# A 3x3 convolution with 2x2 max pooling: another sequence of steps and another order of all instructions

## The chip, the cores and the metric

The kernel runs on one core of a Trainium2 chip. A core has TensorE (PE in the profile; its weight loads are PEld), VectorE (DVE), ScalarE (ACT), GpSimd (POOL) and SyncE (SP), which issues most of the transfers. Each engine executes its own list of instructions strictly in the order in which the program wrote them, and waits at an instruction until the semaphores it needs have come. The metric is the device time of one execution in microseconds (us).

## What is computed

The reference, cut to what matters; the inputs are float32, x is 16 x 64 x 64 x 64, the weight 128 x 64 x 3 x 3, the output 16 x 128 x 32 x 32:

```python
x_pad = np.pad(x, ((0, 0), (0, 0), (pad, pad), (pad, pad)), mode='constant')
...
conv[b, co] += weight[co, ci, kh, kw] * x_pad[b, ci, kh:kh+h, kw:kw+w]
...
output[b, c, i, j] = np.max(conv[b, c, i*pool_size:(i+1)*pool_size,
                                          j*pool_size:(j+1)*pool_size])
```

## The kernel before

**Steps.** Two images lie on the 128 partitions, 64 input channels each (h = 0 and h = 1 in the names). A pair of images is cut into four quarters of 16 input rows, which give 8 rows of pooled output. A quarter of a pair is one step; there are 8 x 4 = 32 steps. Pooling takes the maximum of two neighbouring rows y0 and y1, and later of two neighbouring columns. With g0, g1, g2 for the three rows of the filter, and a, b, c, d for the rows 2i-1 to 2i+2 of the input,

- a K step (13 of them) makes five products: A = (g2-g1) c + g0 a (PAa and PAb), B = (g0-g1) b + g2 d (PBa and PBb), and R = g1 (b+c) (PR); max(y0, y1) is max(A, B) + R. It needs the rows in bf16 (tile kx, cast by the transfer that GpSimd issues) and one row operation, ks = b+c;
- a W step (19) makes four: P2 = (g0+g2-g1)/2 (c-b), P0 = g0 (a-c), P3 = g2 (d-b), P1 = (g0+g2+g1)/2 (b+c); y0 = P2+P0+P1 and y1 = P3-P2+P1, so the maximum is max(P2+P0, P3-P2) + P1. It needs the rows in float32 (tile wx, from transfers that SP issues) and four row operations: we = c-b, wz = a-c, wy = d-b, ws = b+c.

`SEQ` is the sequence of K and W steps; it also decides in which quarter of which pair each lies (`place`, lines 45 to 51).

**Products.** Each product is three matmuls for the three columns of the filter, on 64 partitions, into one bank of PSUM. There are eight banks (`acc`). A token such as `P1.2.0+PBa.3.1:6` in the order is a group of six matmuls: product P1 of W step 2, image 0, in turn with PBa of K step 3, image 1; ":6" names the bank that is taken. The two images' matmuls use different halves of TensorE and run side by side. Below, a *group* is such a token.

**What the other engines do for a step**, by the names in the order (capitals for K, small letters for W):

- ScalarE: `EV`/`ev` copies the first accumulator (A, or P2+P0) to SBUF and frees its bank (line 290); `SE` writes -P2 into a second bank, to which P3 is added (295); `OD`/`od` copies the odd columns to SBUF (303).
- VectorE: `MX`/`mx` takes the maximum of the second accumulator and the copy (299), in place, and only then may PR or P1 be added to it; `CM`/`cm` takes the maximum of even and odd columns, which frees the bank (327), and the second of two images stores the step (344). `KS`, `S` and `E` are the row operations ks, ws and we (260).
- GpSimd: `Z`, `Y` and `e` are wz, wy and we. A row operation there first waits for the last VectorE operation within SBUF that the order has before it (`on_gpsimd`, lines 81 to 83). `L0` to `L5` issue the loads of kx from K step 2 on, two K steps each (L5 one); L0 waits for KS.0.
- SP: `LD.n` loads W step n. It waits for nothing but its place in SP's list, except that LD.1 waits for GM, LD.2 for E.0 and LD.3 for E.1 (line 371); the stores stand in the same list.

**The weights.** At the start wraw, the filter, lands; g0, g1 and g2 are cast, D2 = g2-g1, D0 = g0-g1, GS = g0+g2, and from it GM and GP are made. Each is turned by four transposes on TensorE (`TD2` and so on) into a bank and copied out (`VD2` and so on) to wt. "/V", "/A" and "/P" name VectorE, ScalarE or GpSimd for an operation that can go to either.

**The first rows.** The rows of K step 0 land in float32 (kfirst) and are cast by `XO1`, `XO` (odd rows) and `XE` (even rows); those of K step 1 land in ksecond (`KX2`, issued behind D2) and are cast by `X1` and `X2`.

**The order** of all this is written out by hand as one string of 577 tokens, `ORDER`, from line 420 on; the loop behind it issues them one by one.

```python
    for s in ORDER.split():
        act_left[0] -= on_act(s)
        if s[0] == "P":
...
            for matmuls in zip(*made):
                for matmul in matmuls:
                    matmul()
```

The stores of the last two steps go out per image; those made when ScalarE has at most one of its own operations left go in turn to ScalarE's queue and SP's, behind ScalarE's last operation (lines 309 to 320).

Of the kernel before, what the change touches and what calls it, by code (L numbers as in the profile page):

```python
# [10 lines left out]
def kernel(  # L11
# [404 lines left out]


    ORDER = """  # L420
        D0/V g2 g1/P D2 g0 TD0:1 GS/V TD2:4 KX2 XO1/A TG1:0 VD2/V TG0:2 GP/V XO/A TG2:3 VG0/A
# [9 lines left out]
        od.1.1 MX.2.0 SE.2.0:2 PAb.3.0+P3.2.1 cm.1.1 Y.3 MX.2.1 PR.2.0+P2.3.1:4 EV.3.0 mx.2.1
        P0.2.0+PAa.3.1:0 OD.2.0 S.3 P2.3.0:5+P1.2.1 ev.2.0 CM.2.0 e.4 P3.2.0+PAb.3.1 od.2.1 SE.3.1:3 cm.2.1
        PBa.3.0:7+PR.2.1 mx.2.0 SE.3.0:1 Z.4 PBb.3.0+P0.3.1 OD.2.1 P0.3.0+P3.3.1 CM.2.1 ev.3.1 MX.3.0 Y.4
        P1.2.0+PBa.3.1:6 ev.3.0 LD.8 mx.3.1 P2.4.0:4+PBb.3.1 EV.3.1 E.5 od.2.0 PR.3.0+P1.3.1 SE.4.0:5 KS.4
        cm.2.0 P3.3.0+PAa.5.1:0 Y.5 OD.3.0 MX.3.1 od.3.1 P0.4.0+PAb.5.1 mx.3.0 P3.4.0+PR.3.1 Z.5 cm.3.1
        ev.4.0 P1.3.0+P2.4.1:2 EV.5.1 mx.4.0 OD.3.1 PAa.4.0:3+PAa.4.1:4 L2 S.4 SE.4.1:0 PAb.4.0+PAb.4.1
        od.3.0 CM.3.0 Y.6 CM.3.1 P1.4.0+P0.4.1 EV.4.0 cm.3.0 P2.5.0:6+P3.4.1 LD.9 od.4.0 S.5 EV.4.1
        PBa.4.0:3+P2.5.1:7 cm.4.0 e.7 ev.4.1 PBb.4.0+PBa.4.1:1 mx.4.1 SE.5.0:2 PAa.5.0:4+PBb.4.1 SE.5.1:5
        KS.5 MX.4.0 PAb.5.0+P1.4.1 e.6 MX.4.1 P0.5.0+P0.5.1 EV.5.0 PR.4.0+P3.5.1 S.6 ev.5.1 Z.6
        P3.5.0+P2.6.1:4 ev.5.0 mx.5.1 od.4.1 PBa.5.0:7+PR.4.1 OD.4.0 mx.5.0 Y.7 PBb.5.0+P1.5.1 CM.4.0 OD.4.1  # L440
# [6 lines left out]
        P3.7.0+PR.6.1 od.7.1 S.9 ev.8.1 P0.8.0+P3.8.1 Z.9 cm.7.1 mx.7.0 P3.8.0+PAa.7.1:5 ev.8.0 mx.8.1
        P1.7.0+PAb.7.1 OD.6.1 Y.9 OD.6.0 mx.8.0 P2.9.0:0+P1.8.1 EV.7.1 CM.6.0 e.10 P1.8.0+P2.9.1:2 CM.6.1
        od.8.1 SE.9.0:5 cm.8.1 PAa.9.0:1+PBa.7.1:6 SE.9.1:3 S.10 P0.9.0+PBb.7.1 od.8.0 KS.7 od.7.0
        P3.9.0+P0.9.1 cm.8.0 ev.9.0 Y.10 MX.7.1 PAb.9.0+P3.9.1 ev.9.1 mx.9.0 PBa.7.0:7+P2.10.1:0 EV.9.0 Z.11  # L450
# [5 lines left out]
        od.10.0 P0.11.0+P2.12.1:1 mx.11.1 OD.8.0 Z.13 cm.10.0 P3.11.0+PR.8.1 ev.11.0 CM.8.0
        P2.12.0:3+P1.11.1 OD.8.1 mx.11.0 e.13 SE.12.1:2 PBa.9.0:7+PAb.9.1 CM.8.1 od.11.1 P1.11.0+P3.12.1
        cm.11.1 EV.9.1 KS.9 PBb.9.0+P0.12.1 SE.12.0:6 S.13 od.11.0 P2.13.0:0+PBa.9.1:5 E.14 ev.12.1
        P0.12.0+PBb.9.1 Y.14 cm.11.0 SE.13.0:1 mx.12.1 P3.12.0+P2.13.1:4 ev.12.0 MX.9.1 Z.14 P0.13.0+P1.12.1
        SE.13.1:3 MX.9.0 P3.13.0+PR.9.1 ev.13.0 mx.12.0 e.15 PR.9.0+P0.13.1 OD.9.1 mx.13.0 P1.12.0+P3.13.1  # L460
        CM.9.1 OD.9.0 Y.15 ev.13.1 CM.9.0 P1.13.0+P2.14.1:0 od.12.1 mx.13.1 od.12.0 PAa.11.0:4+P2.15.1:5
        od.13.0 Z.15 cm.12.0 SE.14.1:7 PAb.11.0+P1.13.1 cm.12.1 cm.13.0 PAa.10.0:6+P0.14.1 od.13.1 E.16
        SE.15.1:1 PAb.10.0+P3.14.1 S.15 ev.14.1 P2.14.0:2+P0.15.1 EV.11.0 cm.13.1 S.14 L5 P2.15.0:0+P3.15.1
        ev.15.1 LD.18 e.17 mx.14.1 PBa.10.0:4+PAa.11.1:3 EV.10.0 mx.15.1 SE.14.0:5 PBb.10.0+PAb.11.1
        SE.15.0:6 S.17 P0.14.0+P1.14.1 EV.11.1 KS.10 P0.15.0+P1.15.1 Z.17 MX.10.0 ev.14.0 P3.15.0+PAa.10.1:3
        od.15.1 ev.15.0 cm.15.1 P3.14.0+PAb.10.1 Y.16 od.14.1 mx.15.0 PR.10.0+PBa.10.1:2 EV.10.1 mx.14.0
        Y.17 P2.17.0:0+PBb.10.1 OD.10.0 cm.14.1 P1.15.0+P2.16.1:3 SE.17.0:1 MX.10.1 Z.16 P1.14.0+PAa.12.1:7
        CM.10.0 od.15.0 cm.15.0 P0.17.0+PR.10.1 od.14.0 SE.16.1:4 cm.14.0 P2.16.0:6+PAb.12.1 ev.17.0 S.18
        PBa.11.0:5+P0.16.1 OD.10.1 KS.11 EV.12.1 P3.17.0+P2.17.1:0 S.16 SE.16.0:7 PBb.11.0+P3.16.1 CM.10.1
        e.18 ev.16.1 mx.17.0 P0.16.0+PBa.11.1:2 SE.17.1:3 MX.11.0 P1.17.0+PBb.11.1 Y.18 ev.16.0  # L470
# [77 lines left out]
```

## Time and profile before

| | |
|---|---|
| median of 3 runs | 105.12 us (104.89 to 105.39) |
| the profiled execution | 104.92 us |
| its span, first to last instruction | 103.1 us |
| TensorE busy | 97.2 us (94%) |
| VectorE busy | 90.5 us (88%) |
| ScalarE busy | 81.8 us (79%) |
| GpSimd busy | 67.1 us (65%) |
| granted TensorE clock | full throughout |
| HBM read, written | 17.14 MB, 8.39 MB |

All times below are from the start of the span, in us. A line of a timeline gives the start, the length, the engine, the line of the program, the operation, what it wrote and read, and in brackets how long the engine stood idle before it and what ended that. Operations of one engine overlap a little at their ends, and a matmul is shown longer (0.38) than the time after which the next one is issued (0.11), since they are pipelined.

### The profile page before, as it was taken

The numbers are of one execution on the slowest core, as the hardware profiler recorded it, in microseconds if no ns is written. First come the engines' busy times: TensorE is split into PE (matmuls) and PEld (weight loads), VectorE is DVE, ScalarE is ACT, GpSimd is POOL, SyncE is SP. The second block draws the span as 40 slices with busy tenths as digits, with TensorE's granted clock in tenths as the row PEclk, the third lists the DMA queues.
The fourth block names the chain that finished last, engine by engine and source line by source line (L and its number), as shares of the span: only waits on it lengthen the run. The fifth ranks groups of instructions, "written<-read, shape, count | busy, mean of one in ns | idle before, by whom it ended". The sixth has DMA issues, their size and how long they took to land.

```text
span 103.1 us, 2507 instructions
## 1 busy us (share of the span) xinstructions
PE 97.2 (94%) x888; PEld 55.8 (54%) x888; DVE 90.5 (88%) x178; ACT 81.8 (79%) x177; POOL 67.1 (65%) x76
## 2 busy tenths in 40 slices
...
GB/s 56 353 294 240 214 197 287 223 314 210 404 303 261 152 214 266 245 227 157 213 211 366 317 225 311 199 257 230 379 180 156 236 126 68 199 41 97 113 217 88
DMA packets 12925, 22.81 MB, mean 221 GB/s; under 512 B 1008, under 2 KB 9200, under 8 KB 12912
## 3 DMA queue, kind: packets, MB, share of 16 engines
...
q8 instruction: 7, 0.11, 0.5%
q10 hardware_dynamic: 144, 0.13, 0.4%
q14 instruction: 6, 0.05, 0.2%
HBM read 17.14 MB, written 8.39 MB: 247 GB/s over the span
## 4 chain that ended last, share of the span: by engine, by line
PE 86%; DMA 7%; DVE 2%; ACT 1%; DVEq 0%; issue 0%
PE acc L202 86%; DMA ksecond<-in_x_dram 5%; DMA wraw<-in_weight_dram 3%; DVE wq L391 1%; ACT kx L348 1%; DVE wq L356 0%; DVE o L327 0%; ACT od L303 0%; DVEq L543 0%
## 5 line engine op out<-in xcount | busy, mean ns | idle before, releaser
L202 PEld LDWEIGHTS <-wt 64*128 64x128 bf16 x852 | 53.1, 94 | 38.4 <-issue 1.2
L202 PE MATMUL acc<-kx,wt 64*128 64x504 bf16 (+5 forms) x318 | 57.5, 369 | 0.5 <-ACT kx L348 0.5
L299 DVE TENSOR_TENSOR acc<-acc,ev 128x512 f32<-128x512 f32 x64 | 42.4, 693 | 3.1 <-PE acc L202 2.0
L290 ACT COPY ev<-acc 128x512 f32<-128x512 f32 x64 | 36.6, 592 | 6.2 <-PE acc L202 5.6
L260 POOL TENSOR_TENSOR wz<-wx 128x512 bf16<-128x512 f32 x19 | 24.2, 1274 | 10.8 <-DVE ks L260 4.5
L202 PE MATMUL acc<-wy,wt 64*128 64x504 bf16 (+1 forms) x114 | 29.6, 377 | 0.0
L202 PE MATMUL acc<-wz,wt 64*128 64x504 bf16 (+1 forms) x114 | 29.2, 377 | 0.0
L260 POOL TENSOR_TENSOR wy<-wx 128x512 bf16<-128x512 f32 x19 | 24.1, 1273 | 7.7 <-PE acc L202 3.0
L202 PE MATMUL acc<-we,wt 64*128 64x504 bf16 (+1 forms) x114 | 29.1, 377 | 0.0
L202 PE MATMUL acc<-ws,wt 64*128 64x504 bf16 (+1 forms) x114 | 29.1, 376 | 0.0
L327 DVE TENSOR_TENSOR o<-acc,od 128x256 f32<-128x256 f32 x64 | 25.3, 417 | 2.7 <-ACT od L303 2.3
L303 ACT COPY od<-acc 128x256 f32<-128x256 f32 x64 | 23.0, 382 | 4.4 <-PE acc L202 3.3
L295 ACT ACTIVATE acc<-acc 128x512 f32<-128x512 f32 x38 | 22.0, 586 | 3.4 <-DVE o L327 1.9
L202 PE MATMUL acc<-ks,wt 64*128 64x504 bf16 (+1 forms) x78 | 19.7, 377 | 0.0
L260 POOL TENSOR_TENSOR we<-wx 128x512 bf16<-128x512 f32 x11 | 14.0, 1270 | 5.1 <-PE acc L202 3.4
L260 DVE TENSOR_TENSOR ws<-wx 128x512 bf16<-128x512 f32 x19 | 15.1, 798 | 0.0
L260 DVE TENSOR_TENSOR we<-wx 128x512 bf16<-128x512 f32 x8 | 6.1, 767 | 0.0
L260 DVE TENSOR_TENSOR ks<-kx 128x512 bf16<-128x512 bf16 x13 | 5.4, 419 | 0.1
L105 POOL DMA_DIRECT2D kx<-in_x_dram x6 | 3.5, 589 | 0.0
L482 PE MATMUL acc<-const-bfloat16-1.0 128*128 128x512 bf16 x6 | 2.7, 623 | 0.8 <-PEq L529 0.8
L356 DVE TENSOR_TENSOR wq<-wraw 128x192 bf16<-128x192 f32 x1 | 0.5, 507 | 2.4 <-DMA wraw<-in_weight_dram 2.4
L164 PEld LDWEIGHTS <-wq 128*128 128x128 bf16 x28 | 1.7, 102 | 1.5 <-issue 0.8
...
## 6 DMA issues: line engine op xcount, KB each, us to landing
...
```

The source lines that it names most:

```text
L105: return nc.gpsimd.dma_start(out=ktile(i)[:, lo:hi, :], in_=rows_of(p, lo, hi))
L164: nc.tensor.transpose(turned_rows(m)[:, j, :], wq[:, BLOCKS[m] - 1 + j : BLOCKS[m] + 1 + j, :].rearrange("a b c -> a (b c)"), ident,)
L202: lambda kw=kw, o0=o0, o1=o1, c0=c0, c1=c1: nc.tensor.matmul(dst[:, i0:i1, o0:o1], wt[lo : lo + CI, m0 + kw - h, :], rows(lo, i0, i1, c0, c1),
L260: return engine.tensor_tensor(out=r, in0=t[:, f + a : f + a + 2 * R - 1 : 2, :], in1=t[:, f + b : f + b + 2 * R - 1 : 2, :], op=op,)
L290: nc.scalar.copy(out=ev[g], in_=acc[:, ta[g]])
L295: nc.scalar.mul(acc[:, t], acc[:, ta["w", i, h]], -1.0)
L299: nc.vector.tensor_tensor(out=t, in0=t, in1=ev.pop(g), op=MAX)
L303: nc.scalar.copy(out=od[g], in_=acc[:, tb[g], :, 1::2])
L327: nc.vector.tensor_tensor(out=o[:, h], in0=acc[:, tb[g], :, 0::2], in1=od.pop(g), op=MAX,)
L348: nc.scalar.copy(out=out, in_=in_)
L391: "D2", on_vector(nc.vector.tensor_sub(out=slots(D2), in0=g2, in1=g1))
L482: warm = nc.tensor.matmul(acc[:, n], src[:, 0:128], src, start=True, stop=True, skip_group_check=True)
```

## The change

`SEQ` begins with K and W in turn for eight steps instead of six, and a few W and K change places further on; the numbers of K steps (13) and W steps (19) stay. `ORDER` is a new permutation of the same 577 steps with other banks, in which these operations go to another engine:

- from VectorE to GpSimd: D0 and GP; from GpSimd to ScalarE: g1;
- from VectorE to ScalarE: VG1 and XE; from ScalarE to VectorE: VD0, VG2, VGM, XO and X1;
- we of eleven W steps on VectorE (`E`) and eight on GpSimd (`e`), instead of eight and eleven.

At the start D2 stands ahead of D0 on its engine's list, and L0 ahead of Z.0. At the end P1.18.0 and P1.18.1 form the last group, where before PR.12.0 and P1.18.1 did. The diff, with lines of the order left out:

```diff
-    SEQ = "KWKWKWWKWKWWKWKWWKWKWWKWKWWKWWKW"
+    SEQ = "KWKWKWKWWKWKWWKWWKWKWWKWWKWKWWKW"
...
     ORDER = """
-        D0/V g2 g1/P D2 g0 TD0:1 GS/V TD2:4 KX2 XO1/A TG1:0 VD2/V TG0:2 GP/V XO/A TG2:3 VG0/A
-        PAx.0.0:6+PAx.0.1:7 GM/V PAa.0.0+PAa.0.1 VD0/A VG1/V LD.1 PAb.0.0+PAb.0.1 XE/V VG2/A TGM:2 KS.0
-        TGP:4 E.0 VGM/A PBa.0.0:0+PBa.0.1:1 EV.0.0 Z.0 VGP/V LD.2 PBb.0.0+PBb.0.1 EV.0.1 P2.0.0:4+P2.0.1:3
-        X1/A S.0 L0 PAa.1.0:7+PAa.1.1:2 SE.0.1:5 MX.0.0 Y.0 SE.0.0:6 PAb.1.0+P0.0.1 MX.0.1 X2/A
-        P0.0.0+PAb.1.1 E.1 EV.1.0 PR.0.0+PR.0.1 ev.0.1 S.1 LD.3 EV.1.1 PBa.1.0:7+P3.0.1 KS.1 Z.1 OD.0.1
-        P2.1.0:2+PBa.1.1:3 OD.0.0 CM.0.1 ev.0.0 mx.0.1 P3.0.0+PBb.1.1 SE.1.0:4 Y.1 PBb.1.0+P2.1.1:1 MX.1.1
-        P0.1.0+P1.0.1 CM.0.0 e.2 MX.1.0 SE.1.1:0 P3.1.0+PR.1.1 LD.4 mx.0.0 ev.1.0 PR.1.0+P0.1.1 Y.2 LD.5
...
-        cm.5.0 Z.7 MX.5.1 LD.10 SE.6.0:2 PAa.6.0:0+P3.6.1 cm.5.1 ev.6.1 PAb.6.0+PR.5.1 OD.5.0 e.8 mx.6.1
...
-        P0.7.0+PBb.6.1 MX.6.0 P2.8.0:2+P1.7.1 ev.7.0 LD.11 Z.10 MX.6.1 PR.6.0+P0.8.1 LD.12 SE.8.0:7 LD.13
...
-        PAb.8.0+PAb.8.1 Y.11 mx.10.1 OD.7.0 P3.10.0+P2.11.1:0 CM.7.0 EV.8.1 cm.9.0 P0.10.0+P1.10.1 L4 KS.8
...
-        PR.11.0+P0.17.1 MX.11.1 od.17.0 P2.18.0:6+P3.17.1 Z.18 cm.17.0 ev.17.1 mx.16.1 P3.16.0+PR.11.1
-        SE.18.0:1 mx.17.1 PAa.12.0:0+P1.16.1 OD.11.0 OD.11.1 KS.12 P0.18.0+P1.17.1 CM.11.1 od.16.1 CM.11.0
-        P3.18.0+P2.18.1:2 cm.16.1 od.17.1 mx.16.0 ev.18.0 PAb.12.0+PBa.12.1:5 SE.18.1:4 mx.18.0
-        PBa.12.0:6+PBb.12.1 EV.12.0 cm.17.1 PBb.12.0+P0.18.1 MX.12.1 P1.16.0+P3.18.1 MX.12.0 ev.18.1
-        P1.18.0+PR.12.1 od.16.0 mx.18.1 cm.16.0 OD.12.1 PR.12.0+P1.18.1 CM.12.1 od.18.0 cm.18.0 od.18.1
-        OD.12.0 cm.18.1 CM.12.0
+        g2 D2 D0/P g0 TD2:0 KX2 TG2:1 XO1/A VD2/V TG0:2 GS/V PAx.0.0:6+PAx.0.1:7 VG0/A XO/V TD0:0 GM/V
+        PAa.0.0+PAa.0.1 g1/A VG2/V GP/P PAb.0.0+PAb.0.1 LD.1 XE/A VD0/V TGM:2 EV.0.0 KS.0 TG1:1 E.0
+        PBa.0.0:0+PBa.0.1:3 EV.0.1 L0 VG1/A VGM/V TGP:4 Z.0 LD.2 PBb.0.0+PBb.0.1 VGP/V P2.0.0:4+P2.0.1:2
+        X1/V S.0 SE.0.1:5 PAa.1.0:7+PAa.1.1:1 SE.0.0:6 MX.0.1 Y.0 PAb.1.0+PAb.1.1 X2/A MX.0.0 P0.0.0+P0.0.1
+        EV.1.1 E.1 P3.0.0+P3.0.1 EV.1.0 S.1 ev.0.0 LD.3 PR.0.0+PR.0.1 ev.0.1 KS.1 LD.4 P2.1.0:4+P2.1.1:1 Z.1
+        mx.0.0 OD.0.1 OD.0.0 PBa.1.0:2+PBa.1.1:7 CM.0.1 CM.0.0 SE.1.1:3 PBb.1.0+PBb.1.1 Y.1 mx.0.1 SE.1.0:0
+        P1.0.0+P0.1.1 MX.1.1 P0.1.0+P1.0.1 MX.1.0 ev.1.1 P3.1.0+PR.1.1 od.0.1 ev.1.0 cm.0.1 PR.1.0+PAa.2.1:1
+        KS.3 OD.1.1 L1 od.0.0 PAa.2.0:5+P3.1.1 CM.1.1 KS.2 PAb.2.0+PAa.3.1:4 E.2 PBa.2.0:7+PAb.3.1 mx.1.0
+        Y.2 EV.2.0 PBb.2.0+PAb.2.1 cm.0.0 EV.3.1 mx.1.1 P1.1.0+PBa.2.1:5 OD.1.0 Z.2 LD.5 EV.2.1 CM.1.0
...
+        KS.4 SE.4.1:6 P1.3.0+PAa.5.1:5 E.5 L2 LD.8 od.3.1 cm.2.1 PAb.4.0+P0.4.1 Y.5 mx.4.0 P2.5.0:1+P3.4.1
+        EV.4.0 cm.3.1 ev.4.1 E.6 P1.4.0+PAb.5.1 od.3.0 mx.4.1 PAa.5.0:4+P2.5.1:7 Z.6 od.4.0 EV.5.1 cm.3.0
+        PAb.5.0+PBa.4.1:2 cm.4.0 SE.5.1:0 S.5 PBa.4.0:5+PBb.4.1 LD.9 SE.5.0:3 S.7 PBb.4.0+P0.5.1 LD.10
...
+        PAb.7.0+PAa.6.1:0 S.6 ev.6.0 E.8 PAa.6.0:2+P0.6.1 LD.11 EV.7.0 mx.6.0 P2.7.0:7+P3.6.1 Y.8 OD.5.1
...
+        od.10.1 PAa.8.0:7+PBb.9.1 cm.10.0 ev.11.0 E.12 PAb.8.0+P2.11.1:5 L4 cm.10.1 P2.12.0:4+PAa.8.1:6
...
+        Z.17 cm.15.1 MX.11.0 P2.17.0:1+P3.16.1 ev.16.0 PR.11.0+PAb.12.1 e.18 OD.11.1 mx.16.1 SE.17.0:2
+        P3.16.0+P2.17.1:4 CM.11.1 EV.12.1 KS.12 P0.17.0+P1.16.1 OD.11.0 mx.16.0 SE.17.1:6 Z.18
+        P3.17.0+P2.18.1:3 od.16.1 CM.11.0 ev.17.0 cm.16.1 P1.16.0+P0.17.1 S.17 PBa.12.0:0+PBa.12.1:1 ev.17.1
+        Y.18 mx.17.0 P2.18.0:5+PBb.12.1 od.16.0 SE.18.1:4 cm.16.0 P1.17.0+P3.17.1 MX.12.1 SE.18.0:7
+        PBb.12.0+P0.18.1 mx.17.1 od.17.0 P0.18.0+P3.18.1 ev.18.1 MX.12.0 P3.18.0+P1.17.1 ev.18.0 mx.18.1
+        PR.12.0+PR.12.1 od.17.1 mx.18.0 cm.17.0 OD.12.0 P1.18.0+P1.18.1 OD.12.1 cm.17.1 CM.12.0 od.18.0
+        CM.12.1 od.18.1 cm.18.0 cm.18.1
     """
```

More of the change, by code (lines that the diff above doesn't have):

```diff
@@ L431 @@
[L431 to L440, printed above, removed]
@@ L446 @@
-        P0.7.0+PBb.6.1 MX.6.0 P2.8.0:2+P1.7.1 ev.7.0 LD.11 Z.10 MX.6.1 PR.6.0+P0.8.1 LD.12 SE.8.0:7 LD.13
[L447 to L450, printed above, removed]
@@ L456 @@
[L456 to L460, printed above, removed]
@@ L461 @@
[L461 to L470, printed above, removed]
@@ new lines @@
+        mx.0.0 OD.0.1 OD.0.0 PBa.1.0:2+PBa.1.1:7 CM.0.1 CM.0.0 SE.1.1:3 PBb.1.0+PBb.1.1 Y.1 mx.0.1 SE.1.0:0
+        P1.0.0+P0.1.1 MX.1.1 P0.1.0+P1.0.1 MX.1.0 ev.1.1 P3.1.0+PR.1.1 od.0.1 ev.1.0 cm.0.1 PR.1.0+PAa.2.1:1
+        KS.3 OD.1.1 L1 od.0.0 PAa.2.0:5+P3.1.1 CM.1.1 KS.2 PAb.2.0+PAa.3.1:4 E.2 PBa.2.0:7+PAb.3.1 mx.1.0
+        Y.2 EV.2.0 PBb.2.0+PAb.2.1 cm.0.0 EV.3.1 mx.1.1 P1.1.0+PBa.2.1:5 OD.1.0 Z.2 LD.5 EV.2.1 CM.1.0
+        P2.2.0:6+PBa.3.1:4 MX.2.0 od.1.0 PAa.3.0:1+P1.1.1 LD.6 S.2 SE.2.0:2 PR.2.0+PBb.3.1 E.3 od.1.1
@@ new lines @@
+        P0.2.0+PBb.2.1 cm.1.0 Y.3 OD.2.0 MX.3.1 PAb.3.0+P2.2.1:0 ev.2.0 cm.1.1 P3.2.0+PR.3.1 MX.2.1 Z.3
+        EV.3.0 LD.7 CM.2.0 PBa.3.0:6+P2.3.1:3 OD.3.1 mx.2.0 SE.2.1:1 PBb.3.0+PR.2.1 Y.4 CM.3.1 SE.3.1:7
+        P1.2.0+P0.2.1 MX.3.0 OD.2.1 P2.3.0:4+P0.3.1 E.4 ev.2.1 PR.3.0+P3.2.1 CM.2.1 od.2.0 Z.4 SE.3.0:0
+        cm.2.0 P2.4.0:5+P3.3.1 ev.3.1 mx.2.1 P0.3.0+PAa.4.1:2 S.4 SE.4.0:3 P3.3.0+PAb.4.1 S.3 ev.3.0
+        P0.4.0+P1.2.1 OD.3.0 Z.5 mx.3.1 EV.4.1 P3.4.0+P2.4.1:4 mx.3.0 ev.4.0 PAa.4.0:2+P1.3.1 CM.3.0 od.2.1
@@ new lines @@
+        OD.4.1 CM.4.0 od.5.0 P0.6.0+P2.6.1:6 Y.7 od.5.1 cm.5.0 cm.5.1 PAa.7.0:5+PR.5.1 SE.6.1:3 CM.4.1
+        PAb.7.0+PAa.6.1:0 S.6 ev.6.0 E.8 PAa.6.0:2+P0.6.1 LD.11 EV.7.0 mx.6.0 P2.7.0:7+P3.6.1 Y.8 OD.5.1
+        ev.6.1 PAb.6.0+PAb.6.1 SE.7.0:5 mx.6.1 Z.8 P1.6.0+P2.7.1:6 EV.6.0 CM.5.1 P0.7.0+P1.6.1 od.6.0
+        SE.7.1:2 cm.6.0 P3.7.0+P2.8.1:4 S.8 L3 ev.7.0 PBa.6.0:1+P0.7.1 EV.6.1 KS.6 e.9 mx.7.0 PBb.6.0+P3.7.1
+        od.6.1 ev.7.1 cm.6.1 P2.8.0:7+PBa.6.1:0 SE.8.1:6 mx.7.1 Z.9 P1.7.0+PBb.6.1 LD.12 MX.6.0
@@ new lines @@
+        PBa.5.0:3+P3.8.1 od.7.0 Y.9 cm.7.0 PBb.5.0+P0.8.1 MX.6.1 SE.8.0:5 PR.6.0+P1.7.1 MX.5.0 ev.8.1 e.10
+        P0.8.0+PR.6.1 OD.6.0 mx.8.1 od.7.1 P3.8.0+PAa.7.1:4 ev.8.0 CM.6.0 Y.10 cm.7.1 PR.5.0+P1.8.1 OD.6.1
+        mx.8.0 P2.9.0:2+P2.9.1:1 CM.6.1 od.8.1 Z.10 OD.5.0 cm.8.1 P1.8.0+PAb.7.1 SE.9.1:0 CM.5.0
+        PBa.7.0:6+PBa.7.1:7 S.9 EV.7.1 LD.13 PBb.7.0+P0.9.1 od.8.0 KS.7 SE.9.0:3 Y.11 cm.8.0
+        P2.10.0:4+PBb.7.1 MX.7.0 ev.9.1 P0.9.0+P3.9.1 LD.14 MX.7.1 SE.10.0:5 e.11 PR.7.0+P2.10.1:1 ev.9.0
@@ new lines @@
+        mx.9.1 P0.10.0+PR.7.1 SE.10.1:2 S.10 P3.9.0+P1.9.1 OD.7.0 Z.12 CM.7.0 P3.10.0+P0.10.1 od.9.1 mx.9.0
+        ev.10.0 P2.11.0:6+P3.10.1 Z.11 ev.10.1 mx.10.0 P1.9.0+PAa.9.1:4 OD.7.1 mx.10.1 SE.11.0:1
+        P1.10.0+PAb.9.1 od.9.0 cm.9.1 P3.11.0+P1.10.1 KS.8 EV.9.1 CM.7.1 P0.11.0+PBa.9.1:0 od.10.0 S.11
+        od.10.1 PAa.8.0:7+PBb.9.1 cm.10.0 ev.11.0 E.12 PAb.8.0+P2.11.1:5 L4 cm.10.1 P2.12.0:4+PAa.8.1:6
+        cm.9.0 Y.12 EV.8.0 mx.11.0 LD.15 SE.11.1:3 PBa.8.0:2+PAb.8.1 SE.12.0:7 PBb.8.0+P0.11.1 KS.9 LD.16
@@ new lines @@
+        EV.8.1 e.13 MX.9.1 P0.12.0+P3.11.1 ev.11.1 MX.8.0 P3.12.0+PR.9.1 ev.12.0 E.14 P1.11.0+PBa.8.1:6 S.12
+        PAa.9.0:4+P2.12.1:5 Z.13 mx.11.1 od.11.0 OD.9.1 PR.8.0+PBb.8.1 cm.11.0 CM.9.1 SE.12.1:1
+        PAb.9.0+P1.11.1 Y.14 mx.12.0 OD.8.0 P2.14.0:0+P0.12.1 MX.8.1 od.11.1 EV.9.0 P1.12.0+P3.12.1 Z.14
+        cm.11.1 ev.12.1 CM.8.0 P2.13.0:3+PAa.11.1:4 od.12.0 LD.17 SE.14.0:2 cm.12.0 Y.13 PBa.9.0:5+PAb.11.1
+        mx.12.1 SE.13.0:7 P0.14.0+PR.8.1 EV.11.1 S.14 P0.13.0+P1.12.1 OD.8.1 S.13 ev.14.0 P3.14.0+PAa.10.1:4
```

22 lines of the change are left out of this document (11 added, 11 removed).

## The prediction, made before the changed kernel ran

> **What bounds the kernel now.** I read the chain that ended last first, in order of time, to see which engine sets the end; then the waits, the timelines of VectorE, ScalarE and GpSimd at both ends, the busy times of the long middle, and the transfers. The chain, in time order (start us, length us, what):
>
> ```profile
> 0.74 2.81 DMA wraw<-in_weight_dram
> 3.58 0.51 DVE wq L356
> 4.08 0.77 DVE wq L391
> 4.86 4.80 DMA ksecond<-in_x_dram
> 9.69 0.63 ACT kx L348
> 10.36 87.43 PE acc L202 x805
> 97.82 0.82 PE acc L202 x5
> 98.66 0.38 ACT od L303
> 99.07 0.42 DVE o L327
> ```
>
> From 10.36 to 97.8 the chain is matmuls only: 87.43 us for 805, 0.65 us for a group of six. The change removes no matmul, so it can only move the 10.36, the waits inside, or the end. The busy times of that stretch (PE, PEld, DVE, ACT, POOL, clock, DMA share, GB/s) show that the others fit:
>
> ```profile
> 10.36:97.80 87.44, 87.43 (x811) 51.18 (x811) 81.88 (x162) 73.79 (x162) 62.52 (x54) 1.00 0.81 224
> ```
>
> VectorE has 5.6 us free of 87.4, ScalarE 13.7. What can be gained at most is the wait before 10.36 and one in the last group, whose matmuls stand from 97.4 to 97.82 for mx.18.1. P2.0 is issued from 9.08 and takes one group, to 9.73: the wait before 10.36 is 0.63.
>
> One row of VectorE and two of GpSimd price what happens where both work in SBUF:
>
> ```profile
> 8.70 1.71 DVE L260 TENSOR_TENSOR ws<-wx 128x512 bf16<-128x512 f32 x1
> ```
>
> ```profile
> 3.61 0.87 POOL L387 CAST wq<-wraw 128x192 bf16<-128x192 f32 x1 [1.09 <-DMA wraw<-in_weight_dram]
> 8.60 1.27 POOL L260 TENSOR_TENSOR wz<-wx 128x512 bf16<-128x512 f32 x1 [4.12 <-DVE we L260]
> ```
>
> S.0 takes 1.71 where S alone takes 0.69 (S.1): GpSimd's Z.0 runs from 8.60 to 9.87, and S.0 ends 0.55 behind it. In the same way D2 took 0.84 beside g1's cast and D0 before it 0.51. Whichever comes second waits for the first.
>
> **The start, part by part.** All sums are made against the profiled execution: 104.92 us (span 103.1 and 1.8 around it), 0.20 below the median 105.12.
>
> D2 takes the first place on VectorE: 3.58 + 0.51 = 4.08 instead of 4.84. VD2 ends 0.91 behind D2 now (5.75), so 4.99 then. XO1 still ends at 5.13 (g2, g0 and its transfer stay), and the first products start at 5.18 instead of 5.89. This is worth nothing alone, since what comes next is late:
> - D0 on GpSimd waits for D2 as g1's cast did for D0, and then needs 0.4 (that cast) to 0.9; PE wants it at 5.5. Hidden.
> - GP on GpSimd comes against XO and GM on VectorE. GM waits for it and ends at 6.5 to 6.6, as now (6.59). So LD.1, which waits for GM, is issued at 6.6, as now.
> - g1 (0.54) and the even rows XE (0.41 for 256 elements, 0.61 for 512, so 0.67 for 576) go to ScalarE: VG0, g1, XE end at about 6.8. Covered by VectorE's own row.
> - VectorE does VG2, VD0 (0.42 each) and KS.0 (0.42), to 7.6. E.0 then needs LD.0, issued at 2.67 and 4.9 under way: 7.62 to 8.31. VGM and VGP follow (0.42 each, overlapping by 0.07): 9.02, so P2.0 starts at 9.07. Now it is 9.08: the 0.7 gained in front is gone here, because LD.0 is as late as before.
> - L0's issue goes ahead of Z.0 on GpSimd: 0.7 us from 7.7. E.0 ends at 8.31, so Z.0 is hardly held: 8.46 to 9.73.
> - KX2 is issued behind D2, at 4.09 and not 4.86; with its 4.8 it lands at 8.9, or as late as now (9.67) if it queues behind LD.0.
> - X1 is now VectorE's, ready to start at 8.95, in the middle of Z.0. A cast alone is 0.45 (XE: 0.49 for 576 elements). Held like S.0 it ends 0.45 - 0.14 = 0.31 behind Z.0 (S.0 ended 0.55 behind, of 0.69): 10.04, and PAa.1 starts at 10.09. Not held: P2.0 ends at 9.72 and PAa.1 starts then. Held, and its transfer as late as now: 10.23. No row shows a cast beside GpSimd; the nearest is S.0, so I take 10.09, a gain of 0.27, with ends 0.13 and 0.64.
>
> The Trainium skill's page "GPSIMD Engine Reference", section "Specifications", says that GpSimd shares its SBUF interfaces with VectorE and contends with VectorE instructions in a 2-port mode or with two SBUF inputs. S.0's 1.71 agrees for two inputs. The skill's "VectorE: DVE Perf Modes", section "The perf-mode tier table", puts a float32 copy within SBUF at twice the rate of a two-input operation, and XE's 486 ns for 576 elements beside S.1's 690 for 512 agrees; so X1 should be in a 2-port mode. By these rules X1 is held and the gain is 0.27; were they not to hold here, 0.64.
>
> **Behind the start.** Everything shifts on VectorE: X1, S.0 (0.69, to 10.65), MX.0.1, MX.0.0. Y.0 waits for S.0: 10.77 to 12.05 (1.27). P3.0 stands at the fourth group from PAa.1, 10.09 + 3 x 0.65 = 12.04, so it waits 0.06. E.1 waits for Y.0 (12.05) and for LD.1.
>
> LD.1 is where the moved L0 may hurt. Now LD.1 took 4.6, but LD.2, issued 1.3 ahead of L0, took 6.2, and in 12 to 14 us all transfers together fell to 159 GB/s from 244 in the two us before. L0 moves from 9.81 to 7.7, and so LD.1 stands where LD.2 stood, 1.1 ahead of it. LD.1 lands at 11.2 by its own row, at 12.8 by LD.2's. What it releases: E.1 (0.69), S.1 (0.62 later), KS.1 (0.35 later), then Z.1 (0.13 and 1.27), for P0.1.1, eight groups from PAa.1: 10.15 + 5.2 = 15.35. Back from there, LD.1 costs nothing up to 12.3 and then its whole lateness: 0 or 0.5. I take 0.25, landing at 12.5; the row that stands nearest is LD.2's, but ksecond in front of it is issued 0.77 earlier.
>
> **The middle.** Three subtractions go from GpSimd (11 to 8) to VectorE (8 to 11): 3 x 0.77 = 2.3 us more on VectorE, out of 5.6 free. Hidden while they fall between the maxima that PE waits for. Counting the groups between the product that releases a maximum and the one that needs it, both orders have two or more everywhere but in the last group (29 and 24 times two of 64); two are 1.3 us for one maximum of 0.69. One place is tighter: EV.4.0 and ev.4.1 are released by the same group, and PAa.5.0 needs ev.4.1's bank two groups on: 0.24 from the last issue + 0.52 + 0.58 + 0.05 = 1.39 against 1.30, so 0.09. If the cover goes, at most the 2.3 shows.
> The loads: the new order puts LD.2 to LD.18 13 to 22 groups ahead of their first use (now 11 to 23), L0 to L5 13, 17, 15, 24, 15, 10 (now 13, 15, 15, 20, 21, 10). L4 loses most: 15 x 0.65 = 9.8 us against landings of 7.8 to 9.2. Nothing, but by a little. SP's queue has LD.4 right behind LD.3 in the new order, without a store between; LD.10 and LD.11 go from 12 groups to 22 and 19.
>
> **The end.** Now VectorE's and ScalarE's last work is:
>
> ```profile
> 95.72 2.05 DVE L299 TENSOR_TENSOR acc<-acc,ev 128x512 f32<-128x512 f32 x3
> 97.68 1.15 DVE L327 TENSOR_TENSOR o<-acc,od 128x256 f32<-128x256 f32 x3
> 99.07 0.76 DVE L327 TENSOR_TENSOR o<-acc,od 128x256 f32<-128x256 f32 x2 [0.25 <-ACT od L303]
> ```
>
> ```profile
> 98.66 0.65 ACT L303 COPY od<-acc 128x256 f32<-128x256 f32 x2 [0.36 <-PE acc L202]
> 99.52 0.37 ACTq L320 DMA_DIRECT2D out_dram<-o  x1
> ```
>
> Three maxima in a row end at 97.77 and the last group waits for them, 0.29. In the new order mx.18.0 needs P3.18.0, two groups from the end. With that group's last issue at 0, mx.18.0 runs from 0.24 to 0.93 and P1.18.0, wanted at 0.65, starts at 0.98: 0.33, so +0.04. Behind the last matmul stand two od and two cm as now (0.65, 0.76): from its end to the last cm 1.22 against 1.19. The last store goes out on ScalarE's queue instead of SP's, behind CM.12.1's store: 2.1 to landing (ScalarE's, now) against 1.96: +0.14. Together +0.2.
>
> **Sum.** -0.27 + 0.06 + 0.25 + 0.09 + 0.2 = +0.33: 105.25 for a profiled execution, 105.45 on the median's scale.
>
> **The rivals**, on the median's scale.
> First, as summed: chance 0.45, own range 105.1 to 105.8.
> Second, the start keeps more: X1 is not held (a further -0.37) and LD.1 is in time (-0.25): 104.85. For it: no row shows a cast held. Against: S.0. Chance 0.28; its range goes from 105.1 to 104.4, should the last wait shrink too.
> Third, on the slower side: LD.1 loses against L0. The place is E.1, the point 12.3 us; from there each us costs one. At LD.2's 6.2 it is 0.25 more than summed, 105.7; should it take L0's own 7.9 it lands at 14.5, 2 more. For it: LD.2's row and the fall to 159 GB/s. Against: the fall came 2 us after L0's issue, when LD.1 will be nearly through. Chance 0.17, from 105.7 to 106.5.
> Fourth, VectorE becomes the bound: the three subtractions surface in the middle, +0.7 to +2.3 on the sum, 106.1 to 107.7. Against: the counts above. Chance 0.10.
>
> **Range and chances.** A difference under 0.5% (0.53 us) can't be told from no change. Below 104.59: 0.15 of the second and 0.02 for what I don't see, 0.17. Above 105.65: the third and fourth, and 0.08 of the first for its upper end, 0.35. Between: 0.48. The range 104.5 to 106.2 leaves out the lowest part of the second, the end of the third and most of the fourth.
>
> **What would show it.** First product at 5.2, P2.0 at 9.1, PAa.1 between 9.7 and 10.3; X1's cast 0.9 to 1.1 us long if held, 0.45 if not; LD.1's landing against 12.3 and a wait of E.1 for it; the stretch behind PAa.1 without waits of PE over 0.1; a wait of 0.3 in the last group. I am wrong if PE's start differs from 9.7 to 10.3, if a later load (L4) stops it, or if waits for VectorE appear in the middle.

## The result, and the profile after

The changed kernel takes 105.63 us (median of 6 runs, 105.44 to 106.11); the kernel before, run beside it, takes 105.02 (6 runs, 104.80 to 105.39). The ratio is 1.0059, with a 95% interval of 1.0035 to 1.0082: slower by 0.6%. The forecast was 105.45, in a range of 104.5 to 106.2. All parts below are taken from the profiled executions, 105.44 us (span 103.7) after and 104.92 (span 103.1) before: +0.52.

The chain of the changed kernel that ended last, in order of time (start us, length us, what):

```profile
4.35 1.44 PE acc L164 x12
5.79 0.43 PE acc L202 x6
...
9.19 86.74 PE acc L202 x800
95.93 0.69 DVE acc L299
96.67 0.56 DVE acc L299
97.28 0.41 DVE acc L299
97.88 0.70 DVE o L327 x2
98.88 0.82 DVE o L327 x2
99.70 0.33 DVEq L543
```

It still is TensorE, nearly from end to end, but it runs through other things at both ends. Before, it came through ksecond's transfer and ScalarE's cast into PAa.1; now it passes through the products of PBb and P2.0 (those from 9.19 on), so it is no longer the transfer of ksecond that is last. A pause as short as the 0.16 us that X1 adds in front of PAa.1 (below) does not show in it. At the end it runs through VectorE's maxima from 95.93 on.

The busy times from PAa.1 to the last group (PE, PEld, DVE, ACT, POOL, granted clock, DMA share, GB/s) show the middle:

```profile
10.60:98.00 87.40, 87.25 (x810) 48.63 (x811) 83.48 (x164) 72.93 (x162) 58.80 (x50) 1.00 0.80 225
```

TensorE's lag behind the trace of before is 0.23 at PAa.1 and 0.25 at the 140th group, so the middle costs nothing. VectorE has become 1.6 us busier (83.48, before 81.88) and GpSimd 3.7 less (58.80, before 62.52): the three moved subtractions are hidden.

The start, by the timelines of TensorE, VectorE and GpSimd (start, length, line and operation, tiles, and the idle time ahead of it with its releaser):

```profile
4.35 1.44 PE L164 MATMUL acc<-ident,wq 128*128 128x128 bf16 x12
```

These twelve transposes follow one another every 0.107 us; with full clock (a run below) it is 0.056. The table ahead of the prediction calls the granted clock full throughout. That is so only from 4.57 us on, where the trace of the kernel before has its first record of full clock; here it begins at 5.74.

```profile
7.85 0.68 DVE L260 TENSOR_TENSOR we<-wx 128x512 bf16<-128x512 f32 x1
8.45 0.41 DVE L178 TENSOR_SCALAR wt<-acc 128x512 bf16<-128x512 bf16 x1
9.23 0.42 DVE L178 TENSOR_SCALAR wt<-acc 128x512 bf16<-128x512 bf16 x1 [0.36 <-PE acc L164]
9.57 0.96 DVE L350 CAST kx<-ksecond 128x512 bf16<-128x512 f32 x1
10.45 0.68 DVE L260 TENSOR_TENSOR ws<-wx 128x512 bf16<-128x512 f32 x1
```

```profile
3.75 1.11 POOL L356 TENSOR_TENSOR wq<-wraw 128x192 bf16<-128x192 f32 x1 [1.23 <-DMA wraw<-in_weight_dram]
5.88 0.68 POOL L364 TENSOR_TENSOR wq<-gsum,wraw 128x192 bf16<-128x192 f32 x1 [1.02 <-DVE gsum L360]
8.24 0.70 POOL L105 DMA_DIRECT2D kx<-in_x_dram  x1 [1.67 <-DVE ks L260]
8.96 1.28 POOL L260 TENSOR_TENSOR wz<-wx 128x512 bf16<-128x512 f32 x1
```

The fourth row of VectorE is X1. Alone such a cast takes 0.42 (below); here it takes 0.96, because Z.0 on GpSimd runs from 8.96 to 10.24, and X1 ends 0.29 behind it. PAa.1, which needs X1, starts at 10.59 (10.36 before). Z.0 itself was held back by L0's issue, 8.24 to 8.94: E.0, its other condition, had ended at 8.53. And the row ahead of X1 is VGP, which stood idle for 0.36 until TensorE had made GP's transposes; so P2.0 ran from 9.78 to 10.43 (9.08 to 9.73 before). Without X1 PAa.1 could have started at 10.43; X1 adds 0.16 to that.

The end, by the timelines of VectorE and ScalarE:

```profile
94.66 3.31 DVE L299 TENSOR_TENSOR acc<-acc,ev 128x512 f32<-128x512 f32 x5
97.88 2.15 DVE L327 TENSOR_TENSOR o<-acc,od 128x256 f32<-128x256 f32 x6
```

```profile
98.87 0.65 ACT L303 COPY od<-acc 128x256 f32<-128x256 f32 x2 [0.36 <-PE acc L202]
99.32 1.08 ACTq L320 DMA_DIRECT2D out_dram<-o  x2
```

Five maxima and six column maxima follow each other without a gap from 94.66 to 100.03; before, three and three did. The last group waited 0.36 for its maximum (98.03 instead of 97.67), the last matmul ended at 98.85 (98.63 before), the last column maximum 1.18 behind it (1.20), and the last store landed 3.49 behind it (3.18).

The parts of the +0.52: the start +0.23 (PAa.1), groups behind the start +0.02, the end of the matmuls -0.03, so +0.22 at TensorE's end; the stores behind it +0.31; the rest -0.01.

### The profile page after: what moved, and what is told of

The parts are those of the page before. It is cut to its first block, busy times and chain, and to the rows that moved or that the text cites. A ratio compares the mean times of both kernels' runs of the same rounds, so it can differ in the third digit from the quotient of the medians.

```text
span 103.7 us, 2494 instructions
## 1 busy us (share of the span) xinstructions
PE 97.9 (94%) x888; PEld 53.5 (52%) x888; DVE 91.6 (88%) x182; ACT 79.8 (77%) x175; POOL 64.5 (62%) x74
## 4 chain that ended last, share of the span: by engine, by line
PE 92%; DVE 3%; issue 1%; DVEq 0%
PE acc L202 86%; PE acc L482 3%; PE acc L164 3%; DVE acc L299 2%; DVE o L327 1%; DVEq L543 0%; DVEq L299 0%
## 5 line engine op out<-in xcount | busy, mean ns | idle before, releaser
L202 PEld LDWEIGHTS <-wt 64*128 64x128 bf16 x852 | 50.4, 94 | 40.6 <-issue 0.7
L202 PE MATMUL acc<-kx,wt 64*128 64x504 bf16 (+5 forms) x318 | 56.5, 369 | 0.0
L202 PE MATMUL acc<-wy,wt 64*128 64x504 bf16 (+1 forms) x114 | 28.9, 377 | 0.0
L202 PE MATMUL acc<-wz,wt 64*128 64x504 bf16 (+1 forms) x114 | 28.6, 377 | 0.0
L202 PE MATMUL acc<-we,wt 64*128 64x504 bf16 (+1 forms) x114 | 27.8, 377 | 0.0
L202 PE MATMUL acc<-ks,wt 64*128 64x504 bf16 (+1 forms) x78 | 18.7, 377 | 0.0
L260 DVE TENSOR_TENSOR ws<-wx 128x512 bf16<-128x512 f32 x19 | 14.2, 759 | 0.0
L260 POOL TENSOR_TENSOR we<-wx 128x512 bf16<-128x512 f32 x8 | 10.2, 1270 | 3.8 <-PE acc L202 2.5
L260 DVE TENSOR_TENSOR we<-wx 128x512 bf16<-128x512 f32 x11 | 7.6, 688 | 0.2 <-DMA wx<-in_x_dram 0.2
L164 PE MATMUL acc<-ident,wq 128*128 128x128 bf16 x28 | 2.9, 258 | 0.0
```

Of the source, the lines that this page charges most:

```text
L164: nc.tensor.transpose(turned_rows(m)[:, j, :], wq[:, BLOCKS[m] - 1 + j : BLOCKS[m] + 1 + j, :].rearrange("a b c -> a (b c)"), ident,)
L202: lambda kw=kw, o0=o0, o1=o1, c0=c0, c1=c1: nc.tensor.matmul(dst[:, i0:i1, o0:o1], wt[lo : lo + CI, m0 + kw - h, :], rows(lo, i0, i1, c0, c1),
L260: return engine.tensor_tensor(out=r, in0=t[:, f + a : f + a + 2 * R - 1 : 2, :], in1=t[:, f + b : f + b + 2 * R - 1 : 2, :], op=op,)
```

## The experiments

The runs were made in three groups, each beside the kernel before on the same chip: the first four (before: 105.16 us median), the next four (105.08) and the last three (105.01). A ratio is to the kernel before of its own group.

**L0 later, on the changed kernel.** Its issue goes from ahead of Z.0 to behind S.0.

```diff
-EV.0.1 L0 VG1/A
+EV.0.1 VG1/A
-X1/V S.0 SE.0.1:5
+X1/V S.0 L0 SE.0.1:5
```

> L0 is issued behind S.0 instead of ahead of Z.0; nothing else differs from the changed kernel. Theory one (L0 holds Z.0 on GpSimd, Z.0 holds X1 on VectorE, X1 holds TensorE): Z.0 starts 0.15 behind E.0, near 8.7 instead of 8.96, X1 ends near 10.25, and PAa.1 starts at 10.43, where P2.0 ends, instead of 10.59; LD.1 lands near 11.2 instead of 12.47. Every later group moves with PAa.1, so 0.16 us less in all, 105.47. Theory two (the clock and the transfers alone set the start): Z.0 moves and PAa.1 does not by more than the 0.1 that one run differs from another, 105.6. If X1 is not held by Z.0 at all, its length stays 0.96 wherever Z.0 lies.

105.60 us (11 runs, 105.33 to 106.21), ratio 1.0045 [1.0019, 1.0070]. VectorE and GpSimd:

```profile
9.58 0.42 DVE L178 TENSOR_SCALAR wt<-acc 128x512 bf16<-128x512 bf16 x1 [0.75 <-PE acc L164]
9.92 0.42 DVE L350 CAST kx<-ksecond 128x512 bf16<-128x512 f32 x1
```

```profile
8.63 1.27 POOL L260 TENSOR_TENSOR wz<-wx 128x512 bf16<-128x512 f32 x1 [2.10 <-DVE we L260]
9.85 0.70 POOL L105 DMA_DIRECT2D kx<-in_x_dram  x1
```

Z.0 now starts 0.14 behind E.0 (8.49) and ends at 9.90; X1, behind it, takes 0.42. So L0 did hold Z.0, and Z.0 did hold X1. But PAa.1 started no sooner, at 10.78: VGP waited 0.75 for TensorE and P2.0 went from 10.13 to 10.78. In this execution the trace's first record of full granted clock begins at 6.61 us (5.74 in the changed kernel's), so the transposes in front were slow for longer. LD.1 landed at 11.98, half a microsecond sooner than with L0 early (12.47); other executions, below, scatter as widely.

**The last stores' queues exchanged.**

```diff
-queue = nc.scalar if stored["late"] % 2 else nc.sync
+queue = nc.sync if stored["late"] % 2 else nc.scalar
```

> The last store goes out on SP's queue, as in the kernel before, and that of the image ahead of it on ScalarE's; nothing else differs from the changed kernel. If the queue makes the last landing long (2.28 us on ScalarE's against 1.96 on SP's before), the end comes 0.3 us earlier, 105.3. If it is that four stores follow each other in 0.33 us steps, the landing stays 2.2 to 2.3 and the time within 0.1 of 105.63.

105.72 us (12 runs, 105.22 to 105.92), ratio 1.0049 [1.0028, 1.0071]. The last store took 2.20 to land instead of 2.28, and landed 3.50 behind the last matmul, as in the changed kernel (3.49). The queue is not what costs the 0.31. By chance full clock began at 3.47 here, and the start shows what that is worth: twelve transposes took

```profile
4.32 0.83 PE L164 MATMUL acc<-ident,wq 128*128 128x128 bf16 x12 [0.35 <-DVE wq L391]
```

0.83 instead of 1.44, P2.0 was done at 9.94 (start 9.29), and PAa.1 started at 10.36, held by X1 (9.45 to 10.30). Two runs below had early full clock too and kept little of it.

**Three parts of the start at once:** L0 late as above, X1 on ScalarE, and GP's transposes ahead of PBa.

```diff
-TG1:1 E.0
+TG1:1 TGP:4 E.0
-EV.0.1 L0 VG1/A VGM/V TGP:4 Z.0
+EV.0.1 VG1/A VGM/V Z.0
-X1/V S.0 SE.0.1:5
+X1/A S.0 L0 SE.0.1:5
```

> Three moves at the start of the changed kernel: L0 behind S.0, the cast X1 on ScalarE, and the transposes TGP ahead of PBa instead of behind it. Theory one: VGP no longer waits for TGP behind PBa (0.36), P2.0 starts at 9.56 instead of 9.78 and ends at 10.21; X1 ends at 9.9 on ScalarE; PAa.1 starts at 10.21 instead of 10.59, 0.38 less, 105.25, if the clock goes up at the same time, and up to 0.6 less if it goes up as early as 4.6. Theory two (something else at the start, LD.1 or Y.0, is next): PAa.1 moves, but P3.0 or P0.1.1 waits, and less than 0.2 is left of it.

105.75 us (8 runs, 105.16 to 106.40), ratio 1.0073 [1.0038, 1.0107]: nothing gained, though PAa.1 started at 10.19. The gain is given back at K step 2, whose rows L0 loads. TensorE's timeline and its waits:

```profile
17.28 0.49 PE L202 MATMUL acc<-ks,wt 64*128 64x504 bf16 x2
17.89 0.39 PE L202 MATMUL acc<-kx,wt 64*128 64x512 bf16 x1
```

```profile
PEld L202 <- DMA kx<-in_x_dram: 0.6, 1, 0.6
```

L0 landed at 17.84, where PAa.2.1 needed it at 17.4; TensorE lost 0.29 there against the pace of its groups. Compared with the changed kernel this one was 0.37 ahead at the ninth group and 0.05 at the nineteenth. So the early L0 has its reason in the order: K step 2 comes two groups sooner in it.

**The kernel before, unchanged,** to see how far two executions of one kernel lie apart.

> The kernel before, unchanged, as one of the runs, for its trace at another moment. The granted clock became full at 4.57 in its first trace and at 5.74 in that of the changed kernel. If the moment belongs to the kernel, it is 4.57 again. If it falls by chance, it differs; then the transposes and first products run at half pace as long, but PAa.1 stays at 10.36, since ksecond (landing at 9.67) and X1 decide it, and the time stays 105.0.

105.22 us (12 runs, 104.69 to 105.72), ratio 0.9997 [0.9973, 1.0022]. PAa.1 started at 10.06, against 10.36 in the first trace; ksecond landed at 9.37 instead of 9.67. Full clock began at 4.32 (4.57 in the first trace). The time is the same, but that PAa.1 would stay at 10.36 was wrong. So a single trace tells the start to about 0.3 us, and +0.23 in one pair of traces alone proves nothing.

**X1 alone back on ScalarE.**

```diff
-X1/V S.0
+X1/A S.0
```

> Only the cast X1 goes back from VectorE to ScalarE; L0 stays ahead of Z.0. If X1 on VectorE, held by Z.0, is what makes the start late, X1 begins when ksecond lands (9.3 to 9.4) and ends 0.62 later, near 10.0, and PAa.1 starts where P2.0 ends: 10.43 if the clock goes up at 5.7, earlier if the clock does; 0.16 to 0.4 us less than the changed kernel's 105.63. If VGP and TGP, in front of P2.0, set the start alone, PAa.1 stays within 0.1 of where the clock puts it and the time stays at 105.6.

105.34 us (12 runs, 104.85 to 105.65), ratio 1.0016 [0.9995, 1.0036]: of the 0.6% about two thirds are gone. ScalarE's and VectorE's timelines:

```profile
9.34 0.62 ACT L348 CAST kx<-ksecond 128x512 bf16<-128x512 f32 x1 [0.18 <-DMA ksecond<-in_x_dram]
```

```profile
9.59 1.15 DVE L260 TENSOR_TENSOR ws<-wx 128x512 bf16<-128x512 f32 x1
```

X1 starts when ksecond has landed (9.31) and ends at 9.96, though Z.0 runs beside it. What is held now is S.0, 1.15 instead of 0.68, and nobody needs it at once. PAa.1 (10.45) waited for P2.0 alone.

Full clock began at 3.81 here, and yet PAa.1 is only 0.14 ahead of the changed kernel's. The cast XO started at 5.68, just behind GP on GpSimd (5.61 to 6.29), and took 0.76 instead of 0.29; TensorE waited 0.49 for it. In the run with the queues exchanged XO came ahead of GP. The 0.14 is gone at TensorE's end (98.84, 98.85 in the changed kernel), so the gain rests on the times, and no trace shows all of it.

**X1 on ScalarE and GP's transposes early, L0 left where it is.**

```diff
-TG1:1 E.0
+TG1:1 TGP:4 E.0
-VGM/V TGP:4 Z.0
+VGM/V Z.0
-X1/V S.0
+X1/A S.0
```

> X1 on ScalarE and TGP ahead of PBa; L0 stays ahead of Z.0, so that the rows of K step 2 land near 17.0 and not at 17.84 as with L0 behind S.0, where PAa.2.1 waited 0.29. PAa.1 starts at 10.2, as with all three moves, and this time the gain of 0.38 is kept except for some 0.1 that P0.1.1 waits for Z.1 behind LD.1: 105.3. The rival (whatever is won at the start is lost again by LD.1, which lands at 12.0 to 12.5 beside L0): E.1 waits for LD.1 until 12.4, Z.1 ends at 15.5 and P0.1.1 waits 0.3 or more: 105.5 to 105.6.

105.22 us (12 runs, 105.12 to 105.77), ratio 1.0024 [1.0006, 1.0042]. P2.0 started at 9.60, PAa.1 at 10.25, L0 landed at 16.31 and K step 2 did not wait. E.1 waited 0.38 for LD.1 (landed 12.30), and the group that needs it in the end, P0.1.1, stood at 15.50, where 10.25 + 8 x 0.65 = 15.45: hardly a cost. The last matmul ended at 98.64, as before (98.63); the span is still 0.31 longer, all of it in the last stores. Beyond X1 the transposes bring nothing that the intervals can tell. XO came beside GP here too (0.74).

**One of the last stores left out:** the store of W step 17, the one ahead of the last four. That step's part of the output is not written.

```diff
-elif stored[c, i] == 2:
+elif stored[c, i] == 2 and (c, i) != ("w", 17):
```

> The store of W step 17 (256 KB, issued at 98.66, the one ahead of the last four) is left out, so that part of the output isn't written; nothing else differs from the changed kernel. If the last stores land late (2.2 to 2.3 us instead of 1.96) because they queue behind one another, the last one now lands about 2.0 after its issue, and from the last matmul to the end of the span it is 4.5 us instead of 4.81: 105.35. If the distance of the stores doesn't matter, it stays 4.8 and the time at 105.6.

104.63 us (12 runs, 104.40 to 105.05), ratio 0.9966 [0.9949, 0.9984]: a full microsecond less than the changed kernel. Only 0.28 of it is a sooner landing (3.21 behind the last matmul, not 3.49). Another 0.42 lies behind the landing: the span ended 0.90 after it, not 1.32. The remaining 0.3 no trace shows: the spans of the two profiled executions differ by 0.58. Why the span ends sooner behind the landing, SyncE's waits at the end show, first the changed kernel's, then this one's (us in total, times, longest):

```profile
SPq L543 <- DMA out_dram<-o: 2.3, 1, 2.3
```

```profile
SPq L543 <- DMA out_dram<-o: 1.6, 4, 0.5
```

The transfers use eight semaphores in turn, and at the end SyncE asks all eight, one after another, some 0.06 apart, always in the same order. In both kernels the last store's semaphore is the first to be asked: SyncE passes it at 102.36, behind the landing, and must then ask the other seven, to 102.81. With one transfer fewer the last store's comes last, and the others are asked while it is still under way.

**The first casts of the new start, on the kernel before:** D2 first on VectorE, so that KX2 is issued sooner.

```diff
-D0/V g2 g1/P D2 g0 TD0:1 GS/V TD2:4 KX2
+D2 g2 g1/P D0/V g0 TD2:4 KX2 TD0:1 GS/V
```

> The kernel before with one piece of the change alone: D2 ahead of D0 on VectorE, and its transposes first; L0, X1 and everything else stay. ksecond is issued at 4.2 instead of 4.9. If its landing follows its issue by 4.8 it lands at 9.0 and PAa.1 starts at 9.75, where P2.0 ends: 0.5 less, 104.6. If it queues behind LD.0, as the changed kernel's landing at 9.27 after 5.04 suggests, it lands near 9.3 and PAa.1 starts at 10.0: 0.2 to 0.35 less, 104.85. If the start of the kernel before has another limit, nothing is gained: 105.1.

104.94 us (12 runs, 104.64 to 105.48), ratio 0.9996 [0.9977, 1.0014]. ksecond was issued at 4.28, 0.6 sooner, was 5.41 under way instead of 4.80, and landed at 9.69: nothing. That it queues behind LD.0 fits this, but no run takes LD.0 away.

**Two loads merged, on the kernel before:** LD.4 and LD.5 as one transfer, so that there is one fewer and the last store's semaphore is asked last. All work is done.

```diff
 lo, hi = chunk(q)
+if i == 4:
+    hi = chunk(q + 1)[1]
+    loaded.add(i + 1)
...
-Y.2 LD.5
+Y.2
```

> The kernel before with the loads LD.4 and LD.5 (two neighbouring quarters of one pair, issued one behind the other) as one transfer of both; the work is the same. The transfers take eight semaphores in turn, and at the end SP waits for the eight one by one, 0.065 apart; the last store had the one that SP asks first, so that the other seven waits came behind its landing (101.82 to 102.29). With one transfer fewer the last store has the one asked last. If that is what shortened the kernel without the store of W step 17 by 0.42 more than expected, the end of the span comes 0.9 behind the last landing instead of 1.34: 0.43 less, 104.7. If that came from the missing store itself, the span still ends 1.3 behind the landing: 105.1.

104.72 us (12 runs, 104.36 to 105.34), ratio 0.9964 [0.9944, 0.9984]: faster than both kernels. The span ended 0.89 behind the last landing (1.34 before), and SyncE's line is like that of the run above:

```profile
SPq L546 <- DMA out_dram<-o: 1.2, 4, 0.4
```

By chance this execution also shows what a late LD.1 does. It landed at 12.18, E.1 waited 0.4 for it, and with PAa.1 at 10.09 there was no slack:

```profile
15.77 0.38 PE L205 MATMUL acc<-ws,wt 64*128 64x504 bf16 x1
16.47 0.37 PE L205 MATMUL acc<-wy,wt 64*128 64x512 bf16 x1 [0.32 <-POOL wy L263]
```

TensorE lost 0.55 us, nearly all of it in front of P3.1.0, which needs Y.1. The prediction named P0.1.1 and Z.1 for the new order; Y.1 stands behind Z.1 in the same chain from LD.1.

**The same merge on the changed kernel with X1 on ScalarE.** (The diff is the two above; LD.5 goes from its place in this order.)

> The changed kernel with X1 on ScalarE and the loads LD.4 and LD.5 as one. Against X1 on ScalarE alone (105.34) only the order of the last waits differs: 104.9 if they are worth 0.43, 105.35 if not. Against the kernel before with the same merged loads it should be slower by the 0.3 that the changed kernel's last stores cost: by what is expected of that one, 104.7 to 105.0.

104.97 us (12 runs, 104.59 to 105.72), ratio 0.9994 [0.9969, 1.0018]. The span ended 0.91 behind the landing. Against X1 on ScalarE alone the ratio fell by 0.0022, about half of the 0.43, and the intervals overlap. The new order, mended at both places, equals the old one; with the merge alone, the old one stays 0.3% ahead, as expected, with intervals that overlap slightly.

**Also LD.6 and LD.7 merged, and the store of W step 17 issued in two halves.**

```diff
-if i == 4:
+if i in (4, 6):
...
+elif (c, i) == ("w", 17):
+    nc.sync.dma_start(out=dst[:, h], in_=src[:, h])
...
-EV.3.0 LD.7 CM.2.0
+EV.3.0 CM.2.0
```

> As the changed kernel with X1 on ScalarE and LD.4 and LD.5 as one; besides, LD.6 and LD.7 are one, and the store of W step 17 goes out in two halves, each behind its own column maximum, the first 0.33 earlier. If the last landing is late (3.5 us behind the last matmul, 3.2 in the kernel before) because 768 KB of stores stand in a row from cm.17.1 on, the half that goes earlier takes some of it away: 3.3 to 3.4, 0.1 to 0.2 less than with the store whole. If it is the number of stores in flight, five instead of four make it no better: 3.5 or more.

104.80 us (12 runs, 104.52 to 106.03), ratio 0.9983 [0.9956, 1.0010]. The landing is 3.46 behind the last matmul (3.55 in the run above, 3.49 in the changed kernel): the halves bring under 0.1. This execution also shows what LD.1 costs where the start is early: PAa.1 stood at 10.21, LD.1 landed at 12.56, E.1 waited 0.53 for it, and TensorE lost 0.22 in the group of P0.1.1, which the prediction named. What came last there was not Z.1 but SE.1.1 on ScalarE, behind the column maxima that VectorE does after E.1.

## Why the prediction was right, and where it was wrong

The sum was +0.33, measured +0.52; the direction and the range held, the term of the start had the wrong sign: -0.27 forecast, +0.23 measured. That the sum comes so near is luck. The error of 0.50 at the start is met by 0.38 too much for what stands behind it (LD.1, P3.0 and the middle) and 0.07 for the end of the matmuls, while what follows the last matmul got 0.17 and took 0.31. By the prediction's own sign, TensorE's start between 9.7 and 10.3, its account of the start is wrong (10.59); its signs for X1's length, LD.1, the middle and the last group came true.

How much of the 0.6% each end makes, the traces tell unequally. PAa.1 started at 10.06, 10.09, 10.36 and 10.39 in four executions of the old order (one with D2 first, one with the loads merged) and at 10.36, 10.59 and 10.71 in three of the new one with its start untouched, so the start is later by some 0.3 to 0.4 in the mean, with an overlap. The last landing came 3.18 or 3.19 behind the last matmul in those four, and 3.48 to 3.50 in the kernels of the new order that write all their stores whole (3.55 in one): these 0.31 stand in every trace.

- **D2, first products, KX2: the mechanism was right and worth nothing, as said.** D2 took 3.70 to 4.20. First products came at 5.72, not 5.18: the transposes ran at half rate until 5.74 (0.107 us apart, not 0.056), which the prediction did not count. KX2 was issued at 4.23 and landed at 9.27, between the two landings forecast (8.9 and 9.67).
- **The step that failed: "E.0 ends at 8.31, so Z.0 is hardly held: 8.46 to 9.73", and with it the gain of 0.27.** The slow transposes held VD2 for 0.77 us and GS behind it; GM, beside GP, ended at 6.93 and not at 6.5 or 6.6; VG2, VD0 and KS.0 follow it without a gap, so KS.0 ended at 7.93 and not at 7.6. L0's issue begins 0.31 behind KS.0 (0.31 or 0.32 in all seven executions with L0 early), where 0.1 was forecast; it lay at 8.24 to 8.94 and not at 7.7 to 8.4, Z.0 moved back by 0.5 to 8.96 to 10.24, and X1 with it. The run with L0 late shows the two last links: Z.0 0.14 behind E.0, X1 0.42 long. How much of the 0.5 is the clock's moment stays open. With full clock from 3.47 (the queues exchanged) L0's issue began at 8.01 and Z.0 at 8.73, but with full clock from 3.81 and 4.35 (X1 on ScalarE, without and with the transposes early) at 8.17 and 8.19, since XO was held by GP there.
- **X1 held by Z.0: right, also in size.** 0.31 behind Z.0's end forecast, 0.29 measured. In this trace it costs 0.16, for P2.0 would have let PAa.1 start at 10.43. The times put the price higher: with X1 on ScalarE the ratio falls from 1.0059 to 1.0016, about 0.4 us, but the intervals overlap slightly, and two other kernels with X1 on VectorE stand at 1.0045 and 1.0049. So its size is known only roughly. The rule of the Trainium skill's "GPSIMD Engine Reference", section "Specifications", that GpSimd contends with VectorE instructions in a 2-port perf mode, agrees: 0.96 beside Z.0, 0.42 alone.
- **P2.0 at 9.07: wrong, 9.78.** VGP was forecast as waiting for VectorE's own row only; it waited for GP's transposes, which stand behind PBa on TensorE. P2.0's last matmul was thus issued until 10.43, only 0.1 ahead of X1's end: a second hold beside X1's, and the reason why moving L0 alone gained nothing.
- **LD.1: 0.25 taken, nothing measured** (the lag is 0.24 at P0.1.1 as at the group behind PAa.1). It landed at 12.47 as forecast (12.5) and E.1 waited 0.16 for it. But PAa.1, 0.5 later than forecast, needed P0.1.1 that much later. Where PAa.1 was early, the prediction's point of 12.3 fits: a landing at 12.30 cost hardly anything and one at 12.56 cost 0.22. That L0 is what delays LD.1 was only argued and is not borne out: with L0 early it landed at 11.26 to 12.58 (seven executions, mean 12.1), with L0 late at 11.98 and 12.23, and in the order before at 11.05 to 12.18 (four, mean 11.5). Part of that is its issue, some 0.25 later in the new order. What the early L0 goes with is a late LD.2, issued 0.3 behind it in six of these seven executions and 0.8 in the other: LD.2 was 7.5 to 8.9 under way, against 5.0 and 5.6 with L0 late and 4.9 to 6.2 in the order before. TensorE did not wait for it.
- **Y.0 and P3.0: 0.06 taken, none.** P3.0 was later by more than Y.0.
- **The middle: 0.09 taken, 0.03 measured,** at the place named (PAa.5.0). No load stopped TensorE, L4 neither. The fourth rival, VectorE as the bound, did not come.
- **The wait of the last group: 0.33 taken, 0.36 measured.** But the +0.04 compared it with 0.29 in the old order, and that was a misreading: the last group's six issues there take 0.83 instead of 0.48, so it also waited 0.36, and nothing changed.
- **The last store: +0.14 taken, for the wrong reason; +0.31 measured.** The queue makes no difference (the exchange). Its size is that of a later start of the last stores: from the issue of the 256 KB store ahead of the last four to the last landing it is 3.68 to 3.70 in ten executions of both orders, and 3.75 in one (X1 on ScalarE with the loads merged). The amount behind it is the same in both orders. That store now leaves 0.20 ahead of TensorE's end, before 0.51 ahead: the 0.31. On VectorE its column maxima stand behind five maxima in a row, and that this is why it leaves late was read from the timelines; no run moved them. Leaving that store out took 0.28 off.

The second rival (start kept) fell by X1 and VGP, the third by the slack that the late start left.
